# Six of sixteen sets of W_down's block sums made by accumulating DMAs in DRAM, the other ten spread over the later stages

## The chip, the cores and the metric

The kernel runs on one core of a Trainium2 chip. The core has five engines, each with its own program in its own order: PE (TensorE, matmuls and transposes), DVE (VectorE), ACT (ScalarE), POOL (GpSimd) and SP (SyncE, which here only issues DMAs). Sixteen DMA engines move the data. Engines wait for each other by semaphores. The metric is the device time of one execution in microseconds; smaller is better. Times of the kernel before are the median of three runs.

## What is computed

One layer of a decoder trunk over 512 tokens of width 1024, in float32:

```python
h = RMSNorm(x)
[q k v | B C u | gate_attn gate_conv] = h @ W_in
y_attn = W_attn_out( StickBreakingAttn(q, k, v) )   # 8 heads x 64, strictly causal
y_conv = W_conv_out( B * causal_dwconv3( C * u ) )
m = sigmoid(gate_attn) * y_attn + sigmoid(gate_conv) * y_conv
x = x + RMSNorm(m @ W_o)
x = x + RMSNorm( relu(RMSNorm(x) @ W_up)^2 @ W_down )
x = x + sigmoid(RMSNorm(x) @ W_pg) * (p[i] @ W_pp)
```

W_down is 4096 x 1024. The attention weight of a pair is beta times the product of the keeps between the two positions, which needs a running product along the row and a strictly causal mask.

## The kernel before

**Precision.** Every operand of a matmul is split into a high and a low part (`split`, L63: ACT casts the high part, DVE subtracts for the low part), and `mm3` (L88) multiplies with three matmuls.

**Stages.** On PE they follow each other without a gap by design: the norm and V; the *heads* (four turns of the loop at L412, two heads and one convolution chunk each); *mix* (eight turns at L448, gates and the two output projections); W_o (`rows`, L481); W_up; W_down; the last gate.

**Block sums.** W_down's product is done with seven products of half-size blocks in place of eight (Winograd's form of Strassen's scheme). Four of the seven right-hand operands are sums of W_down's four quarters B11, B12, B21, B22. They depend on nothing but W_down, so they are made long before, and parked in DRAM in `wsum[0..7]` until the W_down stage loads them (`load_t`, L711). There are 16 *sets of sums*, one for each pair of 128-row blocks; each `wsum` tile holds two of them. `make_sums` (L283) makes one set: SP loads two 512 KB blocks, an engine does four `tensor_tensor` of 128x512 (L296), and the two 512 KB results are put on the list `unsaved`. `save_sums` (L276) issues their stores on SP; `make_sums` begins with it, so that a set is stored when the next one is started. The sums are t1 = B12 - B11, t2 = B22 - t1, t3 = B22 - B12, t4 = B21 - t2.

**Who makes them.** Six sets on DVE with lowered priority (`LATE`) in the heads: one ahead of `proj_q(0)`, one ahead of `proj_k(0)`, one ahead of `av` in each of the four turns. Eight sets on POOL, one in each turn of mix. Two on POOL in W_o, at k = 0 and 2.

**What sets the order.** PE and SP run in the order of the code. ACT, DVE and POOL are ordered by a scheduler ahead of the run, from priorities and its own idea of durations; on the chip each engine then runs its list strictly in order, and whatever stands behind a waiting instruction waits too. SP's loads of raw weights go into four buffers (`raws`), so SP runs some projections ahead of PE. Each DMA of SP also waits for the landing of the one eight before it, whose semaphore it takes over.

**One turn of the heads.** PE does `scores` of two heads (L316), the convolution's `conv_u` and `conv_b`, the transposes of head one's weights (`wtrans`, L343), the next q projection, the transposes of head two's, the next k projection, `av` for both, and the next `conv_c`. Between scores and wtrans a head's weights pass ACT (two sigmoids, L329 and L330), POOL (a strictly causal mask on each diagonal block, `affine_select`, L335), and DVE (a running product, L338, and a product, L339), in four blocks. `proj_k` (L309) puts k into the tiles `st` by ACT (L313) and DVE (L314); scores read `st`.

Of the kernel before, what the change touches and what calls it, by code (L numbers as in the profile page):

```python
# [12 lines left out]
ALU = mybir.AluOpType  # L13
# [3 lines left out]
P = 128  # L17
# [6 lines left out]
FF = 4096  # L24
NJ = FF // P // 2
LATE = 150
EPS = 1e-6
CUTS = [[slice(0, 512), slice(512, 1024)]] * 3 + [[slice(0, 512), slice(512, 768), slice(768, 1024)]]
BLK = {3: (0, 512), 2: (512, 384), 0: (896, 128), 1: (1024, 256)}
# [4 lines left out]
def hybrid_block(ctx, tc, x, p, g_pre_mix, w_in, b_gate, w_conv, w_attn_out, w_conv_out, w_o,  # L34
# [43 lines left out]
    def w4(dt=F32):  # L78
        return wts.tile([P, 2, 512], dt, tag="w", name="w4")
# [198 lines left out]
            dst, src = unsaved.pop(0)  # L278
            nc.sync.dma_start(dst, src)

    made = iter(range(NJ))

    def make_sums(eng=None):  # L283
        eng = eng or nc.gpsimd
        save_sums()
        j = next(made)
        q = []
        for h in range(2):
            t = w4()
            nc.sync.dma_start(t, wd[j][h].rearrange("p (c n) -> p c n", c=2))  # L290
            q += [t[:, 0], t[:, 1]]
        dst = wsum[j // 2][:, :, j % 2, :]
        o = [w4(), w4()]
        t1, t2, t3, t4 = (o[i // 2][:, i % 2] for i in range(4))
        for r, x_, y_ in ((t1, q[1], q[0]), (t2, q[3], t1), (t3, q[3], q[1]), (t4, q[2], t2)):
            eng.tensor_tensor(r, x_, y_, op=ALU.subtract)  # L296
        unsaved.extend([(dst[:, 0:2], o[0]), (dst[:, 2:4], o[1])])


# [83 lines left out]
    def conv_u(c, ct):  # L383
        ps = proj(wcols(w_in, 2560 + c * P), hx)
        nc.vector.tensor_tensor(ct, ct, ps, op=ALU.mult)
        y = tm()
        wc = [cols[:, 16 + i * 4 + c:17 + i * 4 + c] for i in range(3)]
        nc.vector.tensor_scalar(y, ct, wc[2], None, op0=ALU.mult)
        for i, d in ((1, 1), (0, 2)):
            nc.vector.scalar_tensor_tensor(y[:, d:S], ct[:, 0:S - d], wc[i], y[:, d:S], op0=ALU.mult, op1=ALU.add)  # L390
        return y
# [9 lines left out]
        nc.scalar.activation(sg, ps, AF.Sigmoid, bias=cols[:, 8 * which + j:8 * which + j + 1])  # L401
        return sg

    with tc.high_priority(-LATE):
        make_sums(nc.vector)
    st = proj_q(0)
    with tc.high_priority(-LATE):
        make_sums(nc.vector)
    proj_k(0, st)
    ct = conv_c(0)  # L410
    sg = [None, None]
    for j in range(4):  # L412
        wa = scores(st[0])
        wb = scores(st[1])
        y = conv_u(j, ct)
        conv_b(j, y)
        ta = wtrans(wa)
        if j < 3:
            st = proj_q(j + 1)
        else:  # L420
            sg[0] = gate(0, 0)
        tb = wtrans(wb)
        if j < 3:
            proj_k(j + 1, st)
        else:
            sg[1] = gate(0, 1)
        of = tm()
        with tc.high_priority(-LATE):
            make_sums(nc.vector)
        av(2 * j, ta, of)  # L430
        av(2 * j + 1, tb, of)
        if j < 3:
            ct = conv_c(j + 1)
# [12 lines left out]
        return lambda k: (oy_h[part][:, k, :], oy_l[part][:, k, :])  # L446

    for j in range(NK):  # L448
        make_sums()
        sa, sc = sg if j == 0 else (next_gate if j == 1 else gate(j, 0), gate(j, 1))  # L450

        def two(t, j=j):
            return [(t[:, 4 * i:4 * i + 4], w[:, j * P:(j + 1) * P].rearrange("(k p) m -> p k m", p=P))
                    for i, w in ((1, w_conv_out), (0, w_attn_out))]

        wo2 = weights(two, [P, NK, P])
        save_sums()
        py = proj(wo2, oyc(1), 4, 4)
        nc.vector.tensor_tensor(sc, sc, py, op=ALU.mult)
        if j == 0:  # L460
            next_gate = gate(1, 0)
        py = proj(wo2, oyc(0), 4, 0)
        nc.vector.tensor_tensor(sa, sa, py, op=ALU.mult)
        nc.vector.tensor_tensor(sa, sa, sc, op=ALU.add)
        split(m_h[j // 4][:, j % 4], m_l[j // 4][:, j % 4], sa)
        if j == 3:
            for t in range(NT):
                nc.sync.dma_start(xr[t // 2][:, t % 2, :], x[t * P:(t + 1) * P, :])
        if j == 6:
            nc.sync.dma_start(pf, p[0].rearrange("(t p) d -> p t d", p=P))  # L470
            nc.sync.dma_start(wpr, w_pp.rearrange("(k p) m -> p k m", p=P))
            split(wph, wpl, wpr)
        if j == 7:
            for kk in range(2):
                ps = bank()
                for t in range(NT):
                    nc.tensor.transpose(ps[:, t * P:(t + 1) * P], pf[:, t, kk * P:(kk + 1) * P], ident)
                split(pt[:, kk], pt[:, 2 + kk], ps)


    def rows(nk, stat, w, tail, chain):  # L481
        acc = {}
        held = {}
        for k in range(nk):
            if k in (0, 2):
                make_sums()
            if k in (1, 3):
                save_sums()
            wk = wrow(w, k)
            if k >= nk - tail:  # L490
                held[k] = wk
                continue
            sh, sl = stat(k)
            for t in range(NT):
                tok = slice(t * P, (t + 1) * P)
                for hf in range(2):
                    if k == 0:
                        acc[t, hf] = bank()
                    cs = slice(hf * 512, (hf + 1) * 512)
                    mm3(acc[t, hf], sh[:, tok], sl[:, tok], wk[0][:, cs], wk[1][:, cs], k == 0, False)  # L500
        for t in range(NT):
            tok = slice(t * P, (t + 1) * P)
            for hf in range(2):
                cs = slice(hf * 512, (hf + 1) * 512)
                for k in range(nk - tail, nk):
                    sh, sl = stat(k)
                    wk = held[k]
                    mm3(acc[t, hf], sh[:, tok], sl[:, tok], wk[0][:, cs], wk[1][:, cs], False, k == nk - 1)
            chain(t, [acc[t, 0], acc[t, 1]])
# [108 lines left out]
    def quarter(m, n, g):  # L618

        return af[g + 4 * n][:, :, m * 256:(m + 1) * 256]  # L620
# [73 lines left out]
    for _, c, n in order:  # L694
        if n == 6 and c + 1 < NJ:
            up_load(c + 1)
        up_mm(c, n)


# [25 lines left out]
    def load_s(n, g):  # L725
        if (n, g) == (1, 0):
            hi, lo = (wts.tile([P, 4, 256], F32R, tag="w", name="s0") for _ in range(2))
        else:
            both = bigt([P, 2, 4, 256], name="sb")
            hi, lo = both[:, 0], both[:, 1]  # L730
        split(hi, lo, quarter(*LEFT[n], g))
        for v in range(4):
            stat[n, 4 * g + v] = hi[:, v], lo[:, v]
        a11, a12 = quarter(0, 0, g), quarter(0, 1, g)
        if n == 1:
            nc.vector.tensor_tensor(a11, quarter(1, 0, g), a11, op=ALU.subtract)
        elif n == 2:
            nc.vector.tensor_tensor(a12, a12, a11, op=ALU.subtract)
        elif n == 6:
            nc.vector.tensor_tensor(a11, quarter(1, 1, g), a11, op=ALU.subtract)  # L740

    back = {}
    xr2 = lambda t: back['x', t // 2][:, t % 2, :]
# [144 lines left out]
```

## Time and profile before

| | |
|---|---|
| median of 3 runs (lowest, highest) | 746.45 us (744.97, 746.55) |
| profiled execution, its own time | 746.06 us |
| its span, first to last instruction | 744.0 us |
| mean granted TensorE clock | 0.993 |
| POOL sums, L296, 10 + 30 instructions | 13.4 + 41.3 us |
| DVE sums, L296, 6 + 18 instructions | 4.1 + 11.6 us |
| DMA: moved in all, mean rate | 132.30 MB, 178 GB/s |

The span is what the trace shows, and 2.06 us of the execution's time lie outside of it. Busy time of an engine is the time in which it executes; an engine other than PE may be idle without any cost as long as PE does not wait for it. In rows of a timeline stand the start in us, the duration, the engine, the line and operation, output and input, and in brackets the idle time before and what ended it. In a table of windows each row is a stretch of the span: its length, then busy time and count of instructions of PE, PE's weight loads, DVE, ACT and POOL, then the granted clock, the DMA engines' busy share and GB/s. In rows of waits stand the total in us, how often, and the longest.

### The profile page before, as it was taken

To read this page: it belongs to the slowest core of one execution; us is meant where nothing else is said; L and a number is where in the kernel's file an instruction comes from. 1 tells how busy PE (TensorE), PEld (TensorE's weight loads), DVE (VectorE), ACT (ScalarE), POOL (GpSimd) and SP (SyncE) were. 2 spreads that over 40 slices of the span, in tenths; PEclk is the share of its full clock that TensorE was granted. 3 is DMA by queue.
4 is the path that set the end of the run, shared out by engine and by line. 5 is a ranking of instruction groups with operands and counts; after the bars stand their busy time and mean duration, and the time that the engine had idled before them with its cause. 6 is when DMAs were issued, how large, how long until landed. Compare 5 with 4: busy or idle time off the path is not lost.

```text
span 744.0 us, 10442 instructions
## 1 busy us (share of the span) xinstructions
PE 730.5 (98%) x3936; PEld 632.4 (85%) x3936; DVE 539.1 (72%) x747; ACT 396.2 (53%) x672; POOL 108.0 (15%) x131
## 2 busy tenths in 40 slices
PE   7999999998999999999999999999999999999997
PEld 6888788887888888878899999999988888888876
DVE  4889898959755424554869879977699878268762
ACT  6555656462533322442855776867776476256531
POOL 0005051347425222200100000000000000001100
PEclk8999999999999999999999999999999999999999
DMA  8393727157599885752244444432555767577311
GB/s 310 126 327 107 221 100 227 54 199 252 178 346 273 254 281 193 269 161 57 106 178 112 115 115 114 118 110 86 168 160 174 224 243 230 174 245 263 128 58 58
DMA packets 112107, 132.30 MB, mean 178 GB/s; under 512 B 4116, under 2 KB 82744, under 8 KB 111032
## 3 DMA queue, kind: packets, MB, share of 16 engines
q1 hardware_dynamic: 111480, 127.44, 53.8%
q10 hardware_dynamic: 576, 4.19, 1.4%
q8 instruction: 31, 0.51, 0.3%
q14 instruction: 20, 0.16, 0.1%
HBM read 108.55 MB, written 23.07 MB: 177 GB/s over the span
## 4 chain that ended last, share of the span: by engine, by line
PE 82%; DVE 6%; DMA 5%; ACT 3%; POOL 2%; issue 1%; SPq 1%; DVEq 0%; POOLq 0%; ACTq 0%
PE ps L89 26%; PE ps L90 26%; PE ps L91 26%; DVE wlo L65 1%; DMA w<-in_w_down_dram 1%; DMA raw<-wsum 1%; PE ps L368 1%; POOL w L296 1%; DMA xin<-in_x_dram 1%; DMA wsum<-w 1%; DMA raw<-in_w_o_dram 1%; ACT whi L64 1%; DVE keep L338 1%; PE ps L354 1%; PE ps L548 1%
## 5 line engine op out<-in xcount | busy, mean ns | idle before, releaser
L65 DVE TENSOR_TENSOR wlo<-raw,whi 128x512 fp32r<-128x512 f32 x120 | 89.4, 776 | 45.8 <-ACT whi L64 19.7
L89 PE MATMUL ps<-h1h,whi 128*128 128x512 f32 x288 | 113.8, 395 | 2.7 <-DVE tmp L395 2.7
L91 PE MATMUL ps<-h1h,wlo 128*128 128x512 f32 x288 | 112.8, 392 | 0.0
L90 PE MATMUL ps<-h1l,whi 128*128 128x512 f32 x288 | 112.7, 391 | 0.0
L64 ACT CAST whi<-raw 128x512 fp32r<-128x512 f32 x120 | 69.1, 638 | 49.6 <-DMA raw<-in_w_in_dram 16.0
L89 PE MATMUL ps<-w,sb 128*128 128x512 f32 x216 | 84.1, 389 | 0.0
L91 PE MATMUL ps<-w,sb 128*128 128x512 f32 x216 | 84.0, 389 | 0.0
L90 PE MATMUL ps<-w,sb 128*128 128x512 f32 x216 | 84.0, 389 | 0.0
L65 DVE TENSOR_TENSOR w<-raw,w 128x1024 fp32r<-128x1024 f32 x56 | 67.7, 1222 | 22.0 <-PE ps L90 11.6
L64 ACT CAST w<-raw 128x1024 fp32r<-128x1024 f32 x56 | 58.4, 1051 | 37.5 <-DMA raw<-wsum 13.4
L125 POOL TENSOR_TENSOR rs<-ms,mhalf 128x1 f32<-128x1 f32 x20 | 14.5, 726 | 409.0 <-DVE ms L121 367.6
L89 PEld LDWEIGHTS ps<-h1h,whi 128*128 128x128 f32 x288 | 54.5, 189 | 13.8 <-DVE tmp L395 2.9
L91 PEld LDWEIGHTS ps<-h1h,wlo 128*128 128x128 f32 x288 | 54.3, 189 | 11.5
L90 PEld LDWEIGHTS ps<-h1l,whi 128*128 128x128 f32 x288 | 54.6, 189 | 11.0
L89 PE MATMUL ps<-h2h,us 128*128 128x256 f32 x224 | 63.5, 283 | 0.0
L90 PE MATMUL ps<-h2l,us 128*128 128x256 f32 x224 | 63.4, 283 | 0.0
L91 PE MATMUL ps<-h2h,us 128*128 128x256 f32 x224 | 63.4, 283 | 0.0
L65 DVE TENSOR_TENSOR us<-raw,us 128x1024 fp32r<-128x1024 f32 x42 | 50.7, 1219 | 7.9 <-ACT us L64 7.7
L64 ACT CAST us<-raw 128x1024 fp32r<-128x1024 f32 x42 | 43.4, 1050 | 19.1 <-DVE raw L647 7.5
L89 PE MATMUL ps<-tb,us 128*128 128x256 f32 x168 | 47.9, 285 | 0.0
L90 PEld LDWEIGHTS ps<-w,sb 128*128 128x128 f32 x216 | 40.5, 188 | 8.5
L89 PEld LDWEIGHTS ps<-w,sb 128*128 128x128 f32 x216 | 40.5, 188 | 8.4
(206 smaller groups left out, 1715.6 us busy)
## 6 DMA issues: line engine op xcount, KB each, us to landing
raw<-in_w_in_dram SPq DMA_DIRECT2D x36, 512.0 KB, 6.9
w<-in_w_down_dram SPq DMA_DIRECT2D x32, 512.0 KB, 4.3
wsum<-w SPq DMA_DIRECT2D x32, 512.0 KB, 3.8
raw<-in_w_up_dram SPq DMA_DIRECT2D x32, 512.0 KB, 4.5
raw<-wsum SPq DMA_DIRECT2D x32, 512.0 KB, 5.1
raw<-in_w_down_dram SPq DMA_DIRECT2D x24, 512.0 KB, 4.3
raw<-in_w_o_dram SPq DMA_DIRECT2D x8, 512.0 KB, 6.0
raw<-in_w_ple_gate_dram SPq DMA_DIRECT2D x8, 512.0 KB, 6.7
```

The lines of the kernel that those rows point to most:

```text
L64: nc.scalar.copy(hi, src)
L65: nc.vector.tensor_tensor(lo, src, hi.bitcast(F32), op=ALU.subtract)
L89: nc.tensor.matmul(ps, lh, rh, start=start, stop=False, skip_group_check=onto)
L90: nc.tensor.matmul(ps, lh, rl, start=False, stop=False, skip_group_check=onto)
L91: nc.tensor.matmul(ps, ll, rh, start=False, stop=stop, skip_group_check=onto)
L125: nc.gpsimd.tensor_tensor(r, m, mhalf, op=ALU.pow)
L296: eng.tensor_tensor(r, x_, y_, op=ALU.subtract)
L338: nc.vector.tensor_tensor_scan(kr, kr, kr, 1.0, op0=ALU.mult, op1=ALU.bypass)
L354: nc.tensor.transpose(ps[:, c0 + (qb - kb) * P:c0 + (qb - kb + 1) * P], w[:, o:o + P], ident)
L368: nc.tensor.matmul(ps[:, kb * P:S], lhs, wt[i][:, c0:c0 + n], start=(kb == 0 and i == 0), stop=(kb == NT - 1 and i == 1))
L548: nc.tensor.transpose(ps[:, i * P:(i + 1) * P], hn1[t][g][:, i * P:(i + 1) * P], ident)
```

## The change

Six sets (`wsum[0]` to `wsum[2]`, two each) are no longer made by an engine. `sums_by_dma(i)` makes two at a time: SP loads the quarters B11 and B22 of two row-block pairs (512 KB each), ACT negates both in place, SP copies B21 from DRAM to DRAM into t4, and stores -B11 into t1 and -B22 into t3 and t2. Then POOL issues four accumulating DMAs of 512 KB, DRAM to DRAM: t1 += B12, t3 += B12, then t2 += t1 and t4 += t2, each of the last two after the landing of what it reads. It is a generator in five pieces; `tick()` starts the next one and moves the running ones on by a piece. It is called ahead of `proj_q(0)`, and twice in each turn of the heads: after the scores, and ahead of `av`.

The other ten sets: two on DVE with lowered priority in the first two turns of mix, four on POOL in the next four, in W_o one on POOL (k = 0) and two on DVE (k = 1, 3), and one on DVE in W_up. t2 and t3 are stored with the other sign; the left-hand side makes up for it (two operations in `load_s`).

```diff
@@ -24,6 +24,7 @@
 FF = 4096
 NJ = FF // P // 2
 LATE = 150
+SETS = 3
 EPS = 1e-6
 CUTS = [[slice(0, 512), slice(512, 1024)]] * 3 + [[slice(0, 512), slice(512, 768), slice(768, 1024)]]
 BLK = {3: (0, 512), 2: (512, 384), 0: (896, 128), 1: (1024, 256)}
@@ -278,7 +279,40 @@
             dst, src = unsaved.pop(0)
             nc.sync.dma_start(dst, src)
 
-    made = iter(range(NJ))
+    made = iter(range(2 * SETS, NJ))
+
+    def quad(r, c, i):
+        r0 = r * FF // 2 + i * 2 * P
+        return w_down[r0:r0 + 2 * P, c * 512:(c + 1) * 512].rearrange("(k p) n -> p k n", p=P)
+
+    def sums_by_dma(i):
+
+        t1, t2, t3, t4 = (wsum[i][:, n] for n in range(4))
+        n11, n22 = w4(), w4()
+        nc.sync.dma_start(n11, quad(0, 0, i))
+        nc.sync.dma_start(n22, quad(1, 1, i))
+        nc.scalar.mul(n11, n11, -1.0)
+        nc.scalar.mul(n22, n22, -1.0)
+        nc.sync.dma_start(t4, quad(1, 0, i))
+        yield
+        for dst, src in ((t1, n11), (t3, n22), (t2, n22)):
+            nc.sync.dma_start(dst, src)
+        yield
+        nc.gpsimd.dma_start(t1, quad(0, 1, i), accum_op=ALU.add)
+        nc.gpsimd.dma_start(t3, quad(0, 1, i), accum_op=ALU.add)
+        yield
+        nc.gpsimd.dma_start(t2, t1, accum_op=ALU.add)
+        yield
+        nc.gpsimd.dma_start(t4, t2, accum_op=ALU.add)
+
+    running, waiting = [], [sums_by_dma(i) for i in range(SETS)]
+
+    def tick():
+        if waiting:
+            running.append(waiting.pop(0))
+        for g in list(running):
+            if next(g, "end") == "end":
+                running.remove(g)
 
     def make_sums(eng=None):
         eng = eng or nc.gpsimd
@@ -292,8 +326,9 @@
         dst = wsum[j // 2][:, :, j % 2, :]
         o = [w4(), w4()]
         t1, t2, t3, t4 = (o[i // 2][:, i % 2] for i in range(4))
-        for r, x_, y_ in ((t1, q[1], q[0]), (t2, q[3], t1), (t3, q[3], q[1]), (t4, q[2], t2)):
-            eng.tensor_tensor(r, x_, y_, op=ALU.subtract)
+        for r, x_, y_, op in ((t1, q[1], q[0], ALU.subtract), (t2, t1, q[3], ALU.subtract),
+                              (t3, q[1], q[3], ALU.subtract), (t4, q[2], t2, ALU.add)):
+            eng.tensor_tensor(r, x_, y_, op=op)
         unsaved.extend([(dst[:, 0:2], o[0]), (dst[:, 2:4], o[1])])
 
 
@@ -401,17 +436,15 @@
         nc.scalar.activation(sg, ps, AF.Sigmoid, bias=cols[:, 8 * which + j:8 * which + j + 1])
         return sg
 
-    with tc.high_priority(-LATE):
-        make_sums(nc.vector)
+    tick()
     st = proj_q(0)
-    with tc.high_priority(-LATE):
-        make_sums(nc.vector)
     proj_k(0, st)
     ct = conv_c(0)
     sg = [None, None]
     for j in range(4):
         wa = scores(st[0])
         wb = scores(st[1])
+        tick()
         y = conv_u(j, ct)
         conv_b(j, y)
         ta = wtrans(wa)
@@ -425,8 +458,7 @@
         else:
             sg[1] = gate(0, 1)
         of = tm()
-        with tc.high_priority(-LATE):
-            make_sums(nc.vector)
+        tick()
         av(2 * j, ta, of)
         av(2 * j + 1, tb, of)
         if j < 3:
@@ -446,7 +478,13 @@
         return lambda k: (oy_h[part][:, k, :], oy_l[part][:, k, :])
 
     for j in range(NK):
-        make_sums()
+        if j < 2:
+            with tc.high_priority(-LATE):
+                make_sums(nc.vector)
+        elif j < 6:
+            make_sums()
+        elif j == 6:
+            save_sums()
         sa, sc = sg if j == 0 else (next_gate if j == 1 else gate(j, 0), gate(j, 1))
 
         def two(t, j=j):
@@ -482,9 +520,9 @@
         acc = {}
         held = {}
         for k in range(nk):
-            if k in (0, 2):
-                make_sums()
-            if k in (1, 3):
+            if k in (0, 1, 3):
+                make_sums(nc.gpsimd if k == 0 else nc.vector)
+            if k == 4:
                 save_sums()
             wk = wrow(w, k)
             if k >= nk - tail:
@@ -694,6 +732,10 @@
     for _, c, n in order:
         if n == 6 and c + 1 < NJ:
             up_load(c + 1)
+            if c == 4:
+                make_sums(nc.vector)
+            if c == 6:
+                save_sums()
         up_mm(c, n)
 
 
@@ -733,11 +775,11 @@
             stat[n, 4 * g + v] = hi[:, v], lo[:, v]
         a11, a12 = quarter(0, 0, g), quarter(0, 1, g)
         if n == 1:
-            nc.vector.tensor_tensor(a11, quarter(1, 0, g), a11, op=ALU.subtract)
+            nc.vector.tensor_tensor(a11, a11, quarter(1, 0, g), op=ALU.subtract)
         elif n == 2:
-            nc.vector.tensor_tensor(a12, a12, a11, op=ALU.subtract)
+            nc.vector.tensor_tensor(a12, a12, a11, op=ALU.add)
         elif n == 6:
-            nc.vector.tensor_tensor(a11, quarter(1, 1, g), a11, op=ALU.subtract)
+            nc.vector.scalar_tensor_tensor(a11, a11, -1.0, quarter(1, 1, g), op0=ALU.mult, op1=ALU.subtract)
 
     back = {}
     xr2 = lambda t: back['x', t // 2][:, t % 2, :]
```

**POOL, ahead of the first heads.** These are POOL's instructions from the four small powers of the first norm on. Before, the masks of heads 0 and 1 (`AFFINE_SELECT`) follow directly:

```order
L125 TENSOR_TENSOR rs<-ms,mhalf 128x1 x4
L335 AFFINE_SELECT beta<-beta 128x128
L335 AFFINE_SELECT keep<-keep 128x128
L335 AFFINE_SELECT beta<-beta 128x128 x2
L335 AFFINE_SELECT keep<-keep 128x128 x2
```

And in the changed program (`wsum_410`, `_411` and `_412` are `wsum[0]` to `wsum[2]`):

```order
L126 TENSOR_TENSOR rs<-ms,mhalf 128x1 x4
L301 DMA wsum_410<-in_w_down_dram 128x2x512
L302 DMA wsum_410<-in_w_down_dram 128x2x512
L304 DMA wsum_410<-wsum_410 128x1024
L306 DMA wsum_410<-wsum_410 128x1024
L301 DMA wsum_411<-in_w_down_dram 128x2x512
L302 DMA wsum_411<-in_w_down_dram 128x2x512
L304 DMA wsum_411<-wsum_411 128x1024
L306 DMA wsum_411<-wsum_411 128x1024
L370 AFFINE_SELECT beta<-beta 128x128
```

All eight accumulations of the first two tiles stand ahead of the first select, though the code starts the second tile's only in the second turn. The third tile's four follow among and behind the selects of heads 0 and 1.

**ACT, between the first k projection and the first scores.** `CAST st` are `proj_k(0)`'s four casts, `COPY tmp` is `conv_c(0)`'s, `ACTIVATE beta` and `keep` the sigmoids. Before:

```order
L313 CAST st<-ps 64x512 x4
L380 COPY tmp<-ps 128x512
L329 ACTIVATE beta<-ps 128x512
L330 ACTIVATE keep<-ps 128x512
L329 ACTIVATE beta<-ps 128x512
```

In the changed program (`w_842` and `w_843` are the blocks B11 and B22 of the third tile, and L294 and L295 negate them):

```order
L348 CAST st<-ps 64x512 x2
L294 ACTIVATE w_842<-w_842 128x1024
L348 CAST st<-ps 64x512
L295 ACTIVATE w_843<-w_843 128x1024
L348 CAST st<-ps 64x512
L415 COPY tmp<-ps 128x512
L364 ACTIVATE beta<-ps 128x512
```

The two negations have moved in among the casts, and each waits for its load.

**SP, from its first load of W_down on.** Before (two sets of sums and the first raw weights):

```order
L290 DMA w_422<-in_w_down_dram 128x1024
L290 DMA w_424<-in_w_down_dram 128x1024
L70 DMA raw<-in_w_in_dram 128x8x128
L279 DMA wsum_410<-w_426 128x2x512
L279 DMA wsum_410<-w_427 128x2x512
L290 DMA w_473<-in_w_down_dram 128x1024
```

In the changed program:

```order
L292 DMA w_422<-in_w_down_dram 128x2x512
L293 DMA w_423<-in_w_down_dram 128x2x512
L296 DMA wsum_410<-in_w_down_dram 128x2x512
L71 DMA raw<-in_w_in_dram 128x8x128 x3
L299 DMA wsum_410<-w_422 128x1024
L299 DMA wsum_410<-w_423 128x1024 x2
L292 DMA w_633<-in_w_down_dram 128x2x512
L293 DMA w_634<-in_w_down_dram 128x2x512
L296 DMA wsum_411<-in_w_down_dram 128x2x512
L71 DMA raw<-in_w_in_dram 128x8x128 x4
L299 DMA wsum_411<-w_633 128x1024
L299 DMA wsum_411<-w_634 128x1024 x2
```

Three raw tiles instead of one now stand ahead of the first stores, and the stores wait for ACT's negations instead of DVE's sums. Behind the last row come `w_842`, `w_843`, the copy into `wsum_412` and one raw tile.

## The prediction

> **What bounds the kernel now.** I read the page's busy lines first, then TensorE's waits, then the windows of the stretches where it falls short.
>
> ```profile
> PE 730.5 (98%) x3936; PEld 632.4 (85%) x3936; DVE 539.1 (72%) x747; ACT 396.2 (53%) x672; POOL 108.0 (15%) x131
> DVE  4889898959755424554869879977699878268762
> PE ps L89 <- DVE tmp L395: 2.7, 1, 2.7
> PE ps L368 <- DVE wtl L65: 0.3, 1, 0.3
> PE ps L327 <- DVE st L314: 0.3, 1, 0.3
> 80.00:100.00 20.00, 19.29 (x92) 15.67 (x91) 17.86 (x28) 15.92 (x33) 6.64 (x12) 1.00 0.70 207
> 160.00:180.00 20.00, 20.00 (x99) 16.92 (x98) 14.40 (x18) 8.47 (x18) 19.84 (x24) 1.00 0.73 232
> 180.00:200.00 20.00, 17.16 (x77) 13.83 (x76) 19.75 (x28) 10.96 (x21) 6.99 (x5) 0.91 0.72 237
> ```
>
> PE is busy 730.5 of a span of 744.0, so work taken off another engine pays only where PE waits for it. The change removes no matmul. Its whole gain must come out of the 13.5 us of idle PE and of matmuls run below full clock. The three waits named above lie in the heads stage. The windows put 0.71 us of idle at 80 to 100 and 2.84 at 180 to 200, where the granted clock is 0.91. What made the large one stands in the rows of POOL, DVE and PE (start, duration, instruction):
>
> ```profile
> 161.03 3.79 POOL L296 TENSOR_TENSOR w<-w,w 128x512 f32<-128x512 f32 x3
> 164.78 0.29 POOL L335 TENSOR_SCALAR_AFFINE_SELECT beta<-beta 128x128 f32<-128x128 f32 x1
> 165.35 1.29 DVE L338 TENSOR_TENSOR_SCAN keep<-keep 128x512 f32<-128x512 f32 x1 [6.21 <-POOL keep L335]
> 184.14 0.69 DVE L395 TENSOR_TENSOR tmp<-ps,tmp 128x512 f32<-128x512 f32 x1
> 184.88 0.80 PE L89 MATMUL ps<-h1h,whi 128*128 128x512 f32 x1 [2.71 <-DVE tmp L395]
> 187.98 0.39 PE L90 MATMUL ps<-h1l,whi 128*128 128x512 f32 x1
> ```
>
> Block sums on POOL hold up the first select, DVE stands 6.21 us for it, its work piles up, and L395 comes 2.71 us late for PE. From 184.88 to 187.98 seven matmuls then start 0.44 us apart; at full clock the starts are 0.23 apart (rows of 53.63 and 53.85 below), so this costs another 3.1 - 7 x 0.23 = 1.5.
>
> **What the change removes.** No POOL sum stands ahead of any select now, and no DVE sum stands in heads 0 to 5. I count 2.84 + 1.5 + 0.71 = 5.1 us regained: **741.0** from the profiled run's 746.06 (span 744.0 and 2.06 around it; the median of the runs shown is 746.45, so the two agree within 0.1%). At most a further 1 us may lie in matmuls slightly late in the same windows. At least 0.7 us is safe.
>
> ```profile
> L296 POOL TENSOR_TENSOR w<-w,w 128x512 f32<-128x512 f32 x30 | 41.3, 1401 | 9.4 <-DMA w<-in_w_down_dram 8.2 <-PE ps L90 0.8
> L296 DVE TENSOR_TENSOR w<-w,w 128x512 f32<-128x512 f32 x18 | 11.6, 692 | 1.4 <-DMA w<-in_w_down_dram 1.1 <-PE ps L90 0.2
> L64 ACT CAST w<-raw 128x1024 fp32r<-128x1024 f32 x56 | 58.4, 1051 | 37.5 <-DMA raw<-wsum 13.4 <-PE ps L91 12.6 <-DMA raw<-in_w_down_dram 7.1
> ```
>
> **What it moves.** POOL goes from 40 sum instructions to 20 (20 x 1.4 = 28 us less). DVE goes from 24 to 20: it loses 24 x 0.69 = 16.6 us in the heads, and gets 8 instructions in the first two turns of mix, 8 in W_o and 4 in W_up. DVE's busy digits in those slices (from 195 us on, eleventh and later) are 7, 5, 5, 4, 2, 4, 5, 5, 4, 8, 6: five or six extra us fit there, and I cost them at nothing. W_up's digits are mostly 7 to 9; four instructions, 2.8 us, fall into one turn, where DVE's own work could be late: 0 to 0.7, taken as 0. The sign changes swap one operation for another of the same shape: nothing. Six negations on ACT, 1.05 each by the cast of that size, cost time only through what they wait for.
>
> **What it adds, and where it meets the path.** Twelve accumulating DMAs go into POOL's in-order program, eight of them ahead of the first select of heads 0 and 1, and their waits are for landings: of SP's stores, and of the accumulation before. Two negations on ACT stand among proj_k(0)'s casts of st, and wait for loads that SP issues late. What these rows show is how much delay is free:
>
> ```profile
> 53.63 0.39 PE L90 MATMUL ps<-h1l,whi 128*128 128x512 f32 x1
> 53.85 0.39 PE L91 MATMUL ps<-h1h,wlo 128*128 128x512 f32 x1
> ...
> 56.70 0.40 PE L326 MATMUL ps<-st 128*128 128x512 f32 x1
> 56.80 0.29 POOL L335 TENSOR_SCALAR_AFFINE_SELECT beta<-beta 128x128 f32<-128x128 f32 x1 [33.59 <-ACT beta L329]
> 64.01 1.14 DVE L339 TENSOR_TENSOR beta<-beta,keep 128x255 f32<-128x255 f32 x2
> 68.91 1.25 PE L354 MATMUL ps<-ident,beta 128*128 128x128 f32 x10
> 54.42 0.59 ACT L313 CAST st<-ps 64x512 fp32r<-64x512 f32 x1 [0.87 <-DVE st L314]
> ```
>
> The first select is at 56.80; the last product of head 0 is the first half of the pair at 64.01, done at about 64.6; PE turns it at 68.91. So POOL may come **4.3 us late, to 61.1**, for nothing. After that each us is one of PE. Head 1's scores read st at 56.70, and the last cast of st stands behind both negations: from the landing of w_843 there follow 1.05 (negation), 0.59 (cast) and some 0.7 (DVE's low part), 2.3 together.
>
> Now the DMA engines, from windows (last two columns: DMA share, GB/s) and two rows of DMA issues:
>
> ```profile
> 12.00:13.00 1.00, 1.00 (x3) 0.70 (x4) 0.93 (x2) 1.00 (x5) 0.00 (x0) 0.50 1.04 412
> 18.00:19.00 1.00, 1.00 (x7) 0.79 (x6) 0.92 (x4) 1.00 (x4) 0.00 (x1) 1.00 0.62 152
> 20.00:30.00 10.00, 10.00 (x52) 8.34 (x50) 8.19 (x21) 5.51 (x14) 0.93 (x1) 1.00 0.01 3
> 40.00:50.00 10.00, 10.00 (x45) 8.26 (x44) 8.39 (x14) 7.40 (x14) 0.00 (x0) 1.00 1.16 324
> 42.00:44.00 2.00, 2.00 (x11) 1.65 (x10) 1.49 (x3) 1.34 (x3) 0.00 (x0) 1.00 1.20 290
> 60.00:70.00 10.00, 10.00 (x51) 8.38 (x51) 9.92 (x18) 5.37 (x12) 6.56 (x12) 1.00 0.01 2
> GB/s 389 389 310 334 298 266 104 22 18 0 0 0 0 0 0 0 0 41 0 0 0 0 0 0 0 0 0 0 20 0 0 0 0 20 0 0 215 389 364 374
> wsum<-w SPq DMA_DIRECT2D x2, 512.0 KB, 2.7
> 9.26 1.70 SPq L290 DMA_DIRECT2D w<-in_w_down_dram  x2
> 29.67 1.57 SPq L279 DMA_DIRECT2D wsum<-w  x2
> ```
>
> Before, SP loads two W_down blocks at 9.26, then stands at its stores until 29.67 since the sums come late, and the engines are idle from 20 to 30 (3 GB/s). The GB/s line (0.4 us slices of 16 to 32) gives 389 for the W_down blocks: 512 KB move in 1.35 us. The raw tiles (512 KB in pieces of 512 B) go at 290: 1.8 us. The two stores that ran alone (300 to 309) took 2.7 us from issue to landing, so 1.4 lies outside of the moving. In both programs the engines are full from SP's first loads on; they run dry at about 18.5 here, after 1.35 + 1.35 + 1.8, so these began to move at 14.0.
>
> In the changed program SP no longer stands. Up to w_843 it moves 14 plain blocks (1.35 each) and 7 raw tiles (1.8): 31.5 us, hence 45.5 without company. The company is POOL's. An accumulating DMA isn't in this trace. Its bounds from the nearest rows: 1.35 us of moving (a copy of that size) and 4.05 (the operand, the old value and the sum each moved by itself). It reads two blocks and writes one where a copy reads one and writes one: 1.5 to 2 passes, 2.0 to 2.7, and I take the middle, **2.35**. I take POOL to cost 1 us an issue (an estimate: SP's pairs take 1.57 to 1.70) and the two queues to share evenly, since the windows at 290 and 412 leave no idle share.
>
> The Trainium skill, "Collectives: The Full Stack", section "The bandwidth ceiling: the fold count and why AG ≠ RS ≠ AR", holds that a reducing transfer pays for two source reads and runs at 1/1.93 of a copy; by it the price would be an estimated 2.6, and the sum below about 752. No accumulating row is in this trace to test it. "DMA: Bandwidth & Descriptors", section "Issuing engines are not separate DMA queues", says that DMAs of POOL and SP end on the same 16 engines; the share of 1.04 at 412 GB/s beside one SP queue agrees that they are already full.
>
> The ledger: t1 of the second set is SP's 17th transfer, 26.1 us of work; with the first set's four accumulations (9.4) it is moved at 14.0 + 35.5 = 49.5 and landed at 50.9. The second set's first accumulation begins to move at about 53. SP has by then moved 3.5 of the 5.4 up to w_843, and moves the other 1.9 at half rate until 57: **w_843 lands at 58.4**, and head 1's scores may start at 60.7, 4.0 late. POOL's second set needs three moves (t1, t3, t2) before its fourth can be issued, 7.05 us of which SP shares the first 10 or so (it has w_843, t4 and a raw tile to move): moved at 65.1, landed at 66.5, and **the first select at 67.5**, against 61.1 + 4.0: 2.4 more. PE loses 6.4, and then runs some matmuls at half clock as at 184.88, 1.5: 741.0 + 6.4 + 1.5 = 748.9, so **749**.
>
> A price higher by 0.35 moves the select by some 3.7 us (5 accumulations on the shared part, and the chain of landings), so the sum turns positive at a price of about 2.1. With 1.35 w_843 lands near 54.8 and POOL is free at 59.4: 741.5. With 2.0 I get 745.4, with 2.7 752.9, with 4.05 about 770.
>
> **The rivals.** (1) **Faster: POOL's queue is empty in time.** If an accumulation moves in less than 1.9 us, or the engines serve a second queue without loss to the first, the first select comes by 61 and all of the 5.1 us stays: 741 to 743. For it: the engines idle from 20 to 30 and 60 to 70 in before, and the second has room for the backlog. Against it: 324 GB/s at a share of 1.16 from 40 to 50, just where the second set falls. (2) **A draw**: a price near 2.1, or a shared loss that about equals the gain: 745 to 747.5. (3) **Much slower: an accumulation costs three passes** or its landing comes several us later than a store's. Each us on one step shifts POOL by about four; at 4.05 POOL is free at about 89 and the time is 760 to 772. (4) **The stall at 182 stays**: DVE's sums in mix slide ahead of the scans of heads 6 and 7, where they wait for late loads. It would take back 4.3 of the gain on any of the other cases; I give it 1 in 10 within them.
>
> **How the numbers follow.** The forecast, POOL held past 61 at a price of 2.2 to 3: 0.41, 748 to 757. Faster: 0.38, likeliest 741 to 743, 744.5 at most. A draw, where 0.2% (1.5 us, about what a measurement can tell) decides: 0.12. Much slower: 0.09. So slower 0.50, same 0.12, faster 0.38. The single likeliest time is 749; its own range is 748 to 757. Cases of both signs hold most of the chance, so the range goes from 740.3 (0.07 left below, if the further 1 us is regained too) to 762 (0.1 above).
>
> **What would show it.** A first AFFINE_SELECT at about 67.5 and a POOL wait there, w_843's negation on ACT at about 58, a PE wait of some 4 us at head 1's scores and a shorter one at wtrans near 69, and a granted clock below 1 in the slices of 60 to 80: right. A first select near 57 to 61 and no PE wait above 1 us before 100: rival 1. No wait L89 <- L395 at 182 shows the gain's main term. The medians of the twelve accumulating rows give the price: 2.35 + 1.4 + the queue's share is above 5 us beside SP. If PE waits in W_o or W_up on DVE, the edits that I cost at nothing were wrong.

## The result and the profile after

| | before | changed |
|---|---|---|
| median, us | 746.07 (4 runs, 744.97 to 746.55) | 780.01 (4 runs, 777.58 to 782.29) |
| span of the profiled run, us | 744.0 | 776.8 |
| mean granted clock | 0.993 | 0.973 |

The changed kernel takes 1.0457 times as long (95% interval 1.0419 to 1.0494), 34 us more. The forecast was 749 us with a range of 740.3 to 762: slower was right, the size was not. Slower had a chance of 0.50 in it, so the direction alone says little.

The busy line of the page, four rows of PE's waits (in all, times, longest; L361 are the scores, which read `st`, and L389 is wtrans) and five windows of the changed kernel:

```profile
PE 737.4 (95%) x3936; PEld 637.2 (82%) x3936; DVE 529.1 (68%) x743; ACT 402.9 (52%) x678; POOL 89.2 (11%) x123
PE ps L361 <- ACT st L348: 10.8, 2, 5.9
PE ps L389 <- DVE beta L374: 9.1, 2, 6.6
PE ps L403 <- ACT wth L65: 3.8, 1, 3.8
PE ps L90 <- DVE tmp L430: 2.7, 1, 2.7
40.00:60.00 20.00, 15.97 (x71) 12.88 (x69) 7.68 (x12) 6.21 (x11) 4.06 (x4) 0.97 0.91 231
60.00:80.00 20.00, 13.27 (x42) 10.44 (x43) 2.23 (x4) 10.37 (x20) 2.03 (x2) 0.60 1.02 243
80.00:100.00 20.00, 10.93 (x42) 8.77 (x41) 9.34 (x14) 3.41 (x6) 10.95 (x20) 0.74 0.83 145
100.00:120.00 20.00, 12.27 (x60) 9.74 (x58) 14.83 (x25) 6.97 (x14) 2.10 (x4) 0.92 0.93 190
180.00:200.00 20.00, 20.00 (x103) 17.11 (x101) 17.24 (x28) 11.46 (x22) 0.46 (x2) 1.00 0.56 172
```

The span grew by 32.8. PE is busy 6.9 longer with the same 3936 matmuls (its granted clock was 0.60 and 0.74 in the two stretches from 60 to 100), and idle 25.9 longer (776.8 - 737.4 = 39.4 against 13.5). The new idle time lies between 40 and 120, in the first turns of the heads. The stretch of 180 to 200, where PE had lost 2.84 us before, is full.

POOL's and ACT's rows there, and the page's two rows on POOL's DMAs (median us to landing last):

```profile
27.14 1.35 POOL L301 DMA_DIRECT2D wsum<-in_w_down_dram  x1 [4.23 <-DMA wsum<-w]
41.53 1.16 POOL L302 DMA_DIRECT2D wsum<-in_w_down_dram  x1 [13.04 <-issue]
42.23 1.35 POOL L304 DMA_DIRECT2D wsum<-wsum  x1
56.86 0.81 POOL L306 DMA_DIRECT2D wsum<-wsum  x1 [13.28 <-DMA wsum<-wsum]
58.18 1.20 POOL L301 DMA_DIRECT2D wsum<-in_w_down_dram  x1 [0.51 <-DMA wsum<-w]
71.61 1.15 POOL L302 DMA_DIRECT2D wsum<-in_w_down_dram  x1 [12.23 <-issue]
72.30 1.33 POOL L304 DMA_DIRECT2D wsum<-wsum  x1
85.80 0.84 POOL L306 DMA_DIRECT2D wsum<-wsum  x1 [12.17 <-DMA wsum<-wsum]
86.36 0.59 POOL L370 TENSOR_SCALAR_AFFINE_SELECT beta<-beta 128x128 f32<-128x128 f32 x1
68.16 1.06 ACT L295 ACTIVATE w<-w 128x1024 f32<-128x1024 f32 x1 [3.93 <-DMA w<-in_w_down_dram]
wsum<-in_w_down_dram POOLq DMA_DIRECT2D x6, 512.0 KB, 11.1
wsum<-wsum POOLq DMA_DIRECT2D x6, 512.0 KB, 10.0
```

The first select is at 86.36 where it was at 56.80 before. POOL's eight accumulations stand ahead of it; over all twelve the median landing is 10 and 11 us after the issue. Four steps follow each other, from an issue to the next one that had to wait for its landing: 27.14 to 41.53, 42.23 to 56.86, 58.18 to 71.61 and 72.30 to 85.80. These 14.4, 14.6, 13.4 and 13.5 us are 55.9 of the 59.2 us from the first issue to the first select. Each tile also has one wait that the prediction did not know: L302 needs nothing of L301, but is issued only when L301 has landed (the row says "issue": nothing in the profile released it).

The negation of w_843 begins at 68.16, when its load lands. That load was issued only at 57.80: SP stood 8.8 us for the landing of one of its own stores, where the prediction had it no longer stand. Without accumulations in the heads (the run "beside W_up" below) it was issued at 44.86.

### The profile page after: what moved, and what is told of

Read it like the earlier page. It is cut to its first block, busy times and chain, and to the rows that moved or that the text cites. A ratio compares the mean times of both kernels' runs of the same rounds, so it can differ in the third digit from the quotient of the medians.

```text
span 776.8 us, 10406 instructions
## 1 busy us (share of the span) xinstructions
PE 737.4 (95%) x3936; PEld 637.2 (82%) x3936; DVE 529.1 (68%) x743; ACT 402.9 (52%) x678; POOL 89.2 (11%) x123
## 4 chain that ended last, share of the span: by engine, by line
PE 66%; DVE 11%; DMA 10%; issue 6%; ACT 4%; POOL 2%; SPq 1%; POOLq 0%; ACTq 0%; DVEq 0%
PE ps L91 21%; PE ps L90 21%; PE ps L92 21%; DVE us L66 4%; DMA raw<-in_w_up_dram 3%; DMA raw<-in_w_in_dram 3%; DMA wsum<-w 2%; PE ps L403 1%; ACT us L65 1%; PE ps L389 1%; DMA raw<-wsum 1%; DMA xin<-in_x_dram 1%; ACT junk L118 1%; DVE wlo L66 1%; DVE raw L684 1%
## 5 line engine op out<-in xcount | busy, mean ns | idle before, releaser
L66 DVE TENSOR_TENSOR wlo<-raw,whi 128x512 fp32r<-128x512 f32 x120 | 83.5, 728 | 65.6 <-ACT whi L65 36.6
L65 ACT CAST w<-raw 128x1024 fp32r<-128x1024 f32 x56 | 58.4, 1052 | 36.9 <-PE ps L92 14.3
L90 PE MATMUL ps<-tb,us 128*128 128x256 f32 x168 | 47.8, 285 | 0.0
L91 PE MATMUL ps<-tb,us 128*128 128x256 f32 x168 | 47.5, 283 | 0.0
L92 PE MATMUL ps<-tb,us 128*128 128x256 f32 x168 | 47.5, 283 | 0.0
```

What stands on the lines that cost most here:

```text
L65: nc.scalar.copy(hi, src)
L66: nc.vector.tensor_tensor(lo, src, hi.bitcast(F32), op=ALU.subtract)
L90: nc.tensor.matmul(ps, lh, rh, start=start, stop=False, skip_group_check=onto)
L91: nc.tensor.matmul(ps, lh, rl, start=False, stop=False, skip_group_check=onto)
L92: nc.tensor.matmul(ps, ll, rh, start=False, stop=stop, skip_group_check=onto)
```

## The experiments

Each row is one change to a kernel; ratios are against the kernel before, run on the same chip. Its median beside them was 744.15, 743.82 or 742.98 us (746.07 beside the changed kernel), so runs are compared by their ratios.

| run | us | ratio (95% interval) |
|---|---|---|
| plain copies for the accumulations | 756.73 (one run) | |
| accumulations beside W_up | 756.58 | 1.0142 (1.0101 to 1.0184) |
| only the ten other sets moved | 740.21 | 0.9948 (0.9929 to 0.9967) |
| probes, some side by side | 750.62 (one run) | |
| one tile instead of three | 741.94 | 0.9981 (0.9967 to 0.9995) |
| probes, one after the other | 773.84 (one run) | |
| each tile behind a turn's selects | 748.92 | 1.0070 (1.0046 to 1.0095) |
| ten moved and two more | 737.60 | 0.9908 (0.9886 to 0.9930) |
| third tile a turn later | 768.05 | 1.0327 (1.0301 to 1.0353) |
| accumulations of B12 in halves | 771.44 | 1.0379 (1.0344 to 1.0415) |

### Plain copies in the accumulations' place

```diff
-        nc.gpsimd.dma_start(t1, quad(0, 1, i), accum_op=ALU.add)
+        nc.gpsimd.dma_start(t1, quad(0, 1, i))
...
```

(and so for t3, t2 and t4)

> The changed kernel with the twelve accumulating DMAs turned into plain copies of the same blocks, from the same place in POOL's program and with the same waits; the additions of six sets are left out. Theory (an accumulation itself holds the DMA engines some 6 us, 4 to 5 times a copy): POOL is free before 61 us, no PE wait on st or beta above 1 us in the heads, and the time is 741 to 745. Rival 1 (DMAs issued by POOL are slow whatever they do, or it is the chain of waits for landings): still 765 or more. Rival 2 (the loads and negations among ACT's casts delay the scores): the waits of PE on st stay, 750 to 760.

756.73: the theory falls, and time and wait are those of rival 2. POOL's rows, and of the pages of the changed kernel and of this run the row of POOL's queue, q0 (packets, MB, and the time that the packets took, as a share of 16 engines' span):

```profile
26.60 0.88 POOL L301 DMA_DIRECT2D wsum<-in_w_down_dram  x1 [3.85 <-DMA wsum<-w]
27.81 0.70 POOL L302 DMA_DIRECT2D wsum<-in_w_down_dram  x1 [0.33 <-DMA wsum<-w]
38.28 0.55 POOL L304 DMA_DIRECT2D wsum<-wsum  x1 [9.76 <-DMA wsum<-in_w_down_dram]
...
70.81 0.54 POOL L306 DMA_DIRECT2D wsum<-wsum  x1 [10.65 <-DMA wsum<-wsum]
71.36 0.31 POOL L370 TENSOR_SCALAR_AFFINE_SELECT beta<-beta 128x128 f32<-128x128 f32 x1
q0 software_dynamic: 2496, 6.29, 5.6%
q0 software_dynamic: 1728, 6.29, 3.1%
```

Some 21 to 23 us of the changed kernel's time go with the addition (780.01 - 756.73; 21 by the ratios, 1.0457 and 756.73/744.15 = 1.0169). Of the spans of 776.8 and 754.7 us the shares are 43.5 and 23.4 us: one accumulation took 3.6 us of the 16 engines, one plain copy 1.95. L302 no longer waits for L301. But even eight plain copies hold POOL until 71, and PE still waits 8.3 us for st (against 10.8): SP's loads are late beside POOL's copies too. The next run shows that the negations and loads by themselves are not the cause.

### The accumulations behind W_o, beside W_up

```diff
+    with tc.issue_after(last_pool[0].ins):   # POOL's last rs of W_o
+        for _ in range(4):
+            for g in gens:
+                next(g, None)
```

(the ticks in the heads now stop after the stores)

> The changed kernel with the twelve accumulations behind POOL's last instruction of W_o, so that they run beside W_up; loads, negations and stores stay in the heads. Theory: heads without the stall and without the one at 182, and W_up has room on the DMA engines for 12 x 6 = 72 us: 740 to 744, faster than before. If they hold up W_up's raw loads: waits of PE in W_up, up to 755. Rival 2 (loads and negations): PE waits on st in the heads, 750 to 760.

Windows of the heads, one of W_up, and PE's two longest waits:

```profile
40.00:60.00 20.00, 20.00 (x95) 16.79 (x94) 11.20 (x17) 13.60 (x26) 3.18 (x7) 1.00 0.81 278
60.00:80.00 20.00, 20.00 (x100) 16.80 (x99) 19.97 (x35) 10.82 (x22) 6.13 (x10) 1.00 0.59 163
430.00:440.00 10.00, 4.28 (x36) 4.08 (x34) 1.31 (x3) 2.66 (x5) 0.81 (x1) 0.83 0.98 190
PE ps L90 <- ACT tmp L722: 8.6, 1, 8.6
PE ps L90 <- ACT tmp L715: 3.6, 2, 2.5
```

Loads, negations and stores alone cost the heads nothing: PE is full there, so the rival of the negations falls. The theory for W_up was wrong: the loss moved there, a little beyond the 755 that I had put beside it. Six raw tiles of W_up issued between 400 and 432 took a median of 12.5 us to land where six between 380 and 412 of the kernel before took 5.0. The engines' share was 0.98 to 1.09 at only 190 to 241 GB/s between 420 and 440: accumulations fill the DMA engines without moving much, by a count that puts down 0.52 MB for one of 512 KB, as for a copy.

### Only the ten other sets moved

```diff
     for j in range(NK):
-        make_sums()
+        if j < 2:
+            with tc.high_priority(-LATE):
+                make_sums(nc.vector)
+        elif j < 6:
+            make_sums()
...
```

(and W_o and W_up as in the change; the heads as before)

> The kernel before with only the ten later sets moved as in the change (two on DVE and four on POOL in mix, three in W_o, one in W_up); the six sets in the heads stay on DVE. Theory: the wait of 2.7 us near 182 and the slow matmuls behind it go, 741 to 742.5. Rival: DVE, which now has sums near 160 as well as its scans, is late there too, and the time stays at 745 to 747.

0.9948: the window of 180 to 200 is full at a clock of 1.00, as the theory had it. This half of the change pays.

### Probes: what one costs

```diff
+        nc.gpsimd.dma_start(probe[0], block[1], accum_op=ALU.add)
+        nc.gpsimd.dma_start(probe[1], block[2], accum_op=ALU.add)
+        nc.gpsimd.dma_start(probe[1], probe[0], accum_op=ALU.add)
...
```

> The kernel before with ten DMAs added on POOL beside W_up, into a scratch block in DRAM: three plain copies of 512 KB, two independent accumulations of 512 KB in rows of 2 KB, two accumulations in rows of 4 KB that depend on each other, a plain copy in rows of 4 KB, an accumulation of 256 KB, and one of 128 KB in pieces of 512 B. Theory: a plain copy lands 3 to 5 us after its issue, an accumulation of 512 KB 8 to 9, the second one is issued only once the first has landed (as in the change), 256 KB about 5; if the price is by row, the 128 KB in 256 pieces cost as much as 512 KB in 256 rows. Rival (only the crowd in the heads made them slow): accumulations land after 4 to 5 us here. Time of the kernel 745 to 750.

> The kernel before with ten DMAs of 512 KB added on POOL beside W_up, each waiting for the one before, so that none runs beside another of POOL's: two plain copies in rows of 2 KB, two accumulations in rows of 2 KB, a plain copy and an accumulation in rows of 4 KB, a plain load into SBUF, an accumulation in SBUF, an accumulation from SBUF into DRAM, and a plain copy in rows of 4 KB. Theory A (the dear thing is that POOL issues it): plain copies land 5 us after their issue, like accumulations in rows of 4 KB; accumulations in rows of 2 KB 7.5. Theory B (the addition is dear): plain copies 3 us, accumulations 7 or more, in rows of 4 KB too. Theory C (DRAM on both sides is dear): the DMAs with SBUF on one side land after 3 us.

POOL's rows, five of the first run (side by side where they can be), then of the second, where each waits for the one before:

```profile
368.16 0.91 POOL L569 DMA_DIRECT2D probes<-in_w_down_dram  x1
369.06 0.73 POOL L570 DMA_DIRECT2D probes<-in_w_down_dram  x1
369.75 0.72 POOL L571 DMA_DIRECT2D probes<-in_w_down_dram  x1
378.11 1.20 POOL L572 DMA_DIRECT2D probes<-in_w_down_dram  x1 [7.64 <-issue]
387.35 1.15 POOL L573 DMA_DIRECT2D probes<-in_w_down_dram  x1 [8.04 <-issue]
```

```profile
395.16 1.15 POOL L572 DMA_DIRECT2D probes<-in_w_down_dram  x1 [8.61 <-DMA probes<-in_w_down_dram]
402.90 0.57 POOL L573 DMA_DIRECT2D probes<-probes  x1 [6.59 <-DMA probes<-in_w_down_dram]
407.34 0.83 POOL L574 DMA_DIRECT2D probes<-probes  x1 [3.86 <-DMA probes<-probes]
```

The row of q0 in narrow windows that hold one DMA of POOL each: the accumulation in rows of 2 KB (second run, 395 to 402.8), the plain copy in rows of 4 KB (second run, 402.8 to 407.1), the accumulation in rows of 4 KB (first run, 395.5 to 401):

```profile
q0 software_dynamic: 272, 0.52, 50.9%
q0 software_dynamic: 144, 0.52, 38.5%
q0 software_dynamic: 144, 0.52, 55.9%
```

Such windows also give the landings: the accumulation in rows of 2 KB took 7.4 (second run, L572) and 7.7 us (first run, L573); in rows of 4 KB 5.2 (first run) and, beside four raw tiles, 5.9 (L574); a plain copy in rows of 4 KB 4.1 (L573) and 3.9 (L578). From SBUF into DRAM the accumulation took 6.4 (L577), and in SBUF 6.5 (beside raw tiles). So theory C falls.

The q0 rows tell the moving from the rest. The shares are 4.0, 1.7 and 3.1 us of the engines (the other accumulation in rows of 2 KB: 4.4). Two plain copies in rows of 2 KB, beside other loads, took 1.3 and 1.5. So the addition makes the moving 1.9 times as long in rows of 4 KB and about three times in rows of 2 KB, where it also goes as 272 packets instead of 144. Theory B holds, with a price that depends on the rows; whether it goes by their number stays open, since the last probes of the first run overlapped. That POOL issues them is not what is dear: its plain copies take 1.3 to 1.7 us of the engines, where the prediction had 1.35 for a load of SP. Their landing after 4 us against the 2.7 of SP's store is a difference of the source too (DRAM, not SBUF), and what makes it is not shown.

The rows above also show the odd wait again: three plain copies of 256 rows are issued back to back, two independent accumulations of 256 rows are not.

### One tile instead of three

```diff
-SETS = 3
+SETS = 1
...
         tick()
+        with tc.high_priority(-LATE):
+            make_sums(nc.vector)
         av(2 * j, ta, of)
```

> The changed kernel with one tile (two sets) made by accumulating DMAs instead of three; the other four sets of the heads are made on DVE ahead of av, as before. Theory (the price of four accumulations in a row, about 30 us from the first issue, is what holds POOL): the last of the four is issued at about 57, as in the changed kernel (56.86), the selects begin by 58, inside their slack of 4.3 us, and the time is 740 to 744. Rival (any accumulation beside the loads of the heads costs PE its loads): 750 or more.

```profile
27.71 1.34 POOL L301 DMA_DIRECT2D wsum<-in_w_down_dram  x1 [7.24 <-DMA wsum<-w]
36.63 1.16 POOL L302 DMA_DIRECT2D wsum<-in_w_down_dram  x1 [7.58 <-issue]
37.33 1.34 POOL L304 DMA_DIRECT2D wsum<-wsum  x1
49.47 0.81 POOL L306 DMA_DIRECT2D wsum<-wsum  x1 [10.80 <-DMA wsum<-wsum]
58.48 0.53 POOL L370 TENSOR_SCALAR_AFFINE_SELECT beta<-beta 128x128 f32<-128x128 f32 x1 [8.20 <-ACT beta L364]
20.00:40.00 20.00, 18.44 (x86) 14.38 (x84) 14.66 (x33) 13.52 (x34) 3.85 (x4) 1.00 1.08 287
40.00:60.00 20.00, 17.84 (x80) 14.15 (x79) 12.00 (x18) 9.72 (x21) 2.13 (x4) 1.00 1.04 244
```

741.94, as the theory had it, though the last accumulation is issued at 49.47 and not at about 57: POOL is free at 50 and waits for its select's data, not the other way round. The four are not free, though. PE is idle 1.6 and 2.2 us in the two windows, where it is full with the ten moved alone, and the kernel is 0.3% slower than that one (0.9981 against 0.9948; the intervals just meet). The rival is right in kind here, and far off in size. Whether the accumulations themselves or the other order of loads and casts cost this was not separated.

### Each tile behind a turn's selects

```diff
         tick()
+        if j < 3:
+            with tc.issue_after(last_pool[0].ins):   # the turn's last select
+                for _ in gens[j]:
+                    pass
         av(2 * j, ta, of)
```

> The changed kernel with the same twelve accumulations, but each tile's four behind the selects of one turn of the heads (tile 0 in turn 0, and so on), so that none stands ahead of a select that is ready. Theory (POOL's order and the crowd before 60 us made the loss): four take some 28 us from 66 on, the next selects are due at 91 and have 4 us of slack, 741 to 748. Rival (accumulations hold up the raw loads wherever they run in the heads): PE waits for weights or st, 755 or more.

1.0070, just above what the theory gave. With the same twelve accumulations the kernel takes some 29 us less than the changed one (1.0070 against 1.0457), so most of the loss is in where and when they stand. Behind a turn's selects they stand ahead of none that is ready, and they no longer run beside the loads ahead of 60 us (L302 follows L301 after 8.4 us here, 14.4 in the changed kernel); which of the two counts for more was not separated. They are still no gain: 749 against 740 for the ten moved alone. PE is idle 2.02 and 2.95 us in 80 to 100 and 160 to 180, where four of them (29 us from 66.46 to the last landing) run into the next turn.

### The third tile a turn later, and halves

```diff
+        count[0] += 1
+        if count[0] == 4:
+            waiting.extend(late)
```

> The changed kernel with the third tile's loads, negations and stores begun one turn later, so that no negation stands among the casts of the first k projection; the eight accumulations of the first two tiles stand ahead of the first select as in the change. Theory (POOL's program decides, and the wait behind the negations lies inside it): PE's waits on st fall from 10.8 to about 5, those on beta grow by as much, the first select moves from 86.4 to no earlier than 78, and the time falls by 3 to 9 us, to 771 to 777. Rival (the two delays add up): the time falls by the whole 10.8 and more, to 766 to 769.

PE's waits:

```profile
PE ps L367 <- ACT st L354: 13.3, 2, 8.1
PE ps L395 <- POOL keep L376: 4.5, 1, 4.5
PE ps L395 <- DVE beta L380: 1.8, 1, 1.8
```

The time fell into the rival's range, but not by its mechanism. Without the negations there PE waits longer for st, since the cast next in line on ACT waits 7.77 us for a raw tile. The first select moved by 1 us, to 85.32. What was gained is behind it: the third tile's accumulations stood among the selects, the last of which began at 99.67 in the change and at 93.58 here. So the wait on st comes from the crowd on the DMA engines, not from which load ACT happens to stand for: with the accumulations beside W_up, negations in place, it was nothing.

```diff
-        nc.gpsimd.dma_start(t1, quad(0, 1, i), accum_op=ALU.add)
-        nc.gpsimd.dma_start(t3, quad(0, 1, i), accum_op=ALU.add)
+        for t in (t1, t3):
+            for k in range(2):
+                nc.gpsimd.dma_start(t[:, k], quad(0, 1, i)[:, k], accum_op=ALU.add)
```

> The changed kernel with each of the six accumulations of B12 issued as two of 128 rows (256 KB) instead of one of 256 rows; the same bytes and sums. Theory (POOL holds the second accumulation of 256 rows until the first has landed, since its queue takes only so many rows): the halves are issued without a gap as far as the stores allow, two or three at once, a landing's latency of about 2 us is saved for each pair, and the first select comes 4 to 10 us earlier: 768 to 776. Rival (the price is only in the moving): no change, 778 to 782.

```profile
27.06 2.71 POOL L303 DMA_DIRECT2D wsum<-in_w_down_dram  x3 [4.89 <-DMA wsum<-w]
38.41 0.84 POOL L303 DMA_DIRECT2D wsum<-in_w_down_dram  x1 [8.64 <-DMA wsum<-in_w_down_dram]
```

Three halves are issued within 2.7 us, the fourth only at 38.41, 0.25 us after the first has landed (38.16). The first select came at 80.54, 5.8 us earlier, and the ratio is 1.0379 against 1.0457. So there is a limit on what POOL has under way, and it was worth about 6 us.

In packets the limit fits every run. An accumulation of 256 rows goes as 272 packets; one of 128 rows, a half, or a plain copy goes as 144. Up to 432 packets of POOL's were under way together (three of 144), never the 544 of two such accumulations, and each wait of a DMA on "issue" ended 0.25 to 0.54 us after the landing that made room. What sets the limit is not shown.

### A version that beats both

```diff
-        with tc.high_priority(-LATE):
-            make_sums(nc.vector)
+        if j > 0:
+            with tc.high_priority(-LATE):
+                make_sums(nc.vector)
...
-            if c == 4:
-                make_sums(nc.vector)
```

(from the kernel with the ten moved; the two sets go to POOL in the last two turns of mix)

> The kernel with only the ten sets moved, with two sets more taken from the places where PE still waits: DVE's set ahead of the first av goes to POOL in mix, and so does the one in W_up. No accumulating DMA. Theory: the losses near 83 and 92 us (about 0.8) and in W_up (1.6) go: 737.5 to 739.5. Rival (they come from elsewhere): 740 as with the ten moved.

737.60, 0.9908 (0.9886 to 0.9930), without any accumulating DMA, as the theory had it; the interval of the ten moved (0.9929 to 0.9967) just meets this one. The window of 80 to 100 is full, and no wait of PE in W_up is left.

## Why the prediction was right in direction and wrong in size

**What bounds the kernel: right.** Only PE's waits counted, and the lower clock beside them. The gain was put at 5.1 us; the ten sets alone gave 0.52%, 3.9 us.

**The edits costed at nothing: nearly right.** Loads, negations and stores cost nothing by themselves (PE full from 40 to 80 with the accumulations away). The set in W_up, taken as 0 with a bound of 0.7, cost PE a little: waits of 0.9 us on DVE's L713 in the changed kernel, and none in the last version, where the set goes to POOL.

**Where it meets the path: right.** POOL's program ahead of the first select and the negation of w_843 were the two places named, and PE waits at both: 9.1 us at wtrans and 5.9 of the 10.8 us at the scores. The other 4.9 stand behind a raw tile that came late (ACT's cast of it at 56.78), which the prediction did not name. Nothing speaks against the slack of 4.3 us: with one tile the first select came 1.7 us later than before, at 58.48, and PE did not wait for it.

**The price of an accumulation: wrong, and this is the step that failed first.** I took 2.35 us of moving, the middle of 1.5 and 2 passes of a copy of 1.35, plus 2.4 of issue and landing. The pass was nearly right (POOL's plain copies took 1.3 to 1.7 us beside W_up, 1.95 in the heads), and so were the 2.4 in rows of 4 KB (4.1 - 1.7). The number of passes was not: 3.1 us in rows of 4 KB, 4.0 to 4.4 in rows of 2 KB, and 3.6 on average in the changed kernel. By the prediction's own steps (752.9 at 2.7, about 770 at 4.05) this turns the 749 into some 764. I judged what the DMA does by counting passes without a row of one; the three passes of rival 3 came true for the six in rows of 2 KB, a case to which I gave 0.09 and which lies for the most part beyond the range.

The Trainium skill, "Collectives: The Full Stack", section "The bandwidth ceiling: the fold count and why AG ≠ RS ≠ AR", led to an estimated 2.6. In rows of 4 KB the trace agrees with its factor of 1.93: 1.7 to 3.1 us is 1.9 times. In rows of 2 KB the price was well above it.

**The engines' sharing: right in kind, too small, and the second step that failed.** Even sharing with SP's queue was assumed, and that SP no longer stands. At a price of 3.6 even sharing gives 2 x 3.6 + 2.4 = 9.6 us for a step; the four in the chain took 13.4 to 14.6. SP's loads beside accumulations took 12.5 us in W_up instead of 5.0, and in the heads SP stood 8.8 us ahead of w_843's load, which landed just before 68.16 instead of at 58.4. This does not need the addition: for plain copies of 1.95 the ledger would have had about 745, and 756.73 was measured. So about half of what is missing, from some 764 to 780, is not in the price.

**Rows left out of the ledger.** Two things in that rest were tried. The limit on packets: the halves gave back 0.8% (1.0457 to 1.0379). And I had the third tile's accumulations begin after the second's without a price, though the order shows them among the selects of heads 0 and 1; a turn later the ratio is 1.0327. The two were not tried together, so it is not shown that they make up the rest. The first select came at 86.36 instead of 67.5.

**The rivals.** "Much slower" came nearest, with its mechanism, and beyond its 772. The stall at 182 did not stay.

## What to carry to other kernels

Before work is moved from an engine to DMAs, measure one such DMA in its own form, from the queue that must issue it, alone and beside the loads of that stage: counted passes were wrong by a factor of 1.5 here (2.35 against 3.6), and a step of such a chain beside other loads by about two (13.4 to 14.6 us against 2 x 2.35 + 2.4 = 7.1). A DMA that waits for a landing blocks all that stands behind it on its engine, so look at the order for what the scheduler put there; against the kernel with the ten moved alone, twelve accumulations among and ahead of selects cost 5.1%, the same twelve behind them 1.2%, and four 0.3%. And try the parts of a change apart: one half of this one was worth 0.5%, and 0.9% with two sets more of the same kind.

## What the runs showed of the hardware

- An accumulating DMA of 512 KB issued by POOL landed after 7.4 to 7.7 us in rows of 2 KB and 5.2 in rows of 4 KB; beside SP's loads after 7 to 14. With SBUF on one side it was no cheaper (6.4 to 6.5).
- Of the 16 engines it took 4.0 to 4.4 us in rows of 2 KB and 3.1 in rows of 4 KB; a plain copy of POOL's took 1.3 to 1.7.
- While they ran, the DMA engines were full (share 0.98) at 190 GB/s, where loads of SP reach 412 at 1.04.
- A second accumulation of 256 rows was never issued before the first had landed, in any run; 256 and 128 rows went together, and three of 128. Of POOL's packets at most 432 were under way together.
- PE's granted clock was 0.60 and 0.74 in the two stretches of 20 us from 60 to 100 of the changed kernel, in which PE was idle 6.7 and 9.1 us.
